# A two-layer decoder trunk: where the operands of its matmuls start in SBUF

## The chip, the cores and the metric

The kernel runs on one core of one Trainium2 chip. The metric is the time of one execution on the device, in microseconds (us). Before the change it took 2255.49 us, the median of three runs (2255.02 to 2256.84).

A core has five engines that work side by side and wait for each other by semaphores: TensorE (PE in the profile; its weight loads have a row of their own, PEld), VectorE (DVE), ScalarE (ACT), GpSimd (POOL) and SyncE (SP), which here only issues DMAs. Operands lie in SBUF, on-chip memory of 128 partitions; a tile occupies the same range of byte addresses in each partition. Matmul results go to PSUM.

## What is computed

Two layers, one sequence of 256 tokens, width 2048, everything in float32. Each layer is a token mixer (forgetting attention in layer 0, sliding-window attention in layer 1) and a gated ConvFFN, each with its input modulated by the conditioning vector and followed by a layer norm:

```python
for i in range(DEPTH):
    mod = c_act @ ada_w[i] + ada_b[i]
    sh1, sc1, g1, sh2, sc2, g2 = jnp.split(mod[:, None, :], 6, axis=-1)
    h = x * (1.0 + sc1) + sh1
    y = fox_attention(h, ...) if i % N_MIXERS == 0 else swa_attention(h, positions, ...)
    x = layer_norm(DEEPNORM_ALPHA * x + (1.0 + g1) * y, ln_mix_g[i], ln_mix_b[i])
    h = x * (1.0 + sc2) + sh2
    y = conv_ffn(h, ffn_w_up[i], ffn_conv_w[i], ffn_conv_b[i], ffn_w_down[i])
    x = layer_norm(DEEPNORM_ALPHA * x + (1.0 + g2) * y, ln_ffn_g[i], ln_ffn_b[i])
```

`conv_ffn` multiplies by `w_up` (2048 x 11264), convolves over three tokens, gates one half with the SiLU of the other, and multiplies by `w_down` (5632 x 2048). Nearly all of the work is in these products and in the projections into and out of the attentions.

## The kernel before

**Matmuls in three terms.** Each float32 operand is split into a rounded part (type float32r, which PE takes in one pass) and a residual: a = ah + al. A product is ah·bh + ah·bl + al·bh. For weights, ACT rounds a block `w` into `wh` (line 276) and DVE subtracts to get `wl` (line 287). The modulated input h lies transposed in one tile, `hHL`, 16 blocks of 128 rows, each with 256 columns of the rounded part and 256 of the residual (`hH`, `hL`). The gated values of the FFN lie in tiles `gT` of pool `gp`, and the attention's outputs in `oT`: blocks 0 to 11 in `gp`, blocks 12 to 15 in `hHL` itself, which is free by then (`o_tile`).

**A matmul has a stationary and a moving operand.** The stationary one (128 x 128, 512 bytes per partition) is loaded by a weight load, PEld; the moving one (256 or 512 columns, 1024 or 2048 bytes per partition) then streams past it. The load for the next matmul runs beside the present one. All go through `mm` (line 76). In a form like `wd<-hHL,wh` the name ahead of the arrow is the PSUM tile:

- `wd` (`w_stationary`, FFN up-projection): weights stationary, `hHL` moving. For each pair of 128-row blocks eight matmuls of 512 columns with `wh` (both halves of h at once) and then eight of 256 with `wl`. 22 column blocks of 512 and 8 pairs in each layer: 352 pairs.
- `ws` (`w_mm`, q and k of the first attention): weights stationary, `hHL` moving, 16 matmuls of 256 columns with `wh` and 8 with `wl` for each pair.
- `xs` (`x_mm`: v of the first attention, all of the second attention's input, the output projections, the FFN's down-projection): `hHL`, `oT` or `gT` stationary, weights moving; eight matmuls of 512 columns with `wh` and four with `wl` for each pair. The down-projection has 176 pairs, the two output projections 32 each, the second attention's input 40. The first attention's input has 96 pairs, two thirds of them `ws`; 45 of the 96 are in the opening.

Every pair streams 6144 columns.

**What sets the order.** The kernel's own planner issues a pair at a time: `stream` issues the load of `w` on SP's queue, the rounding on ACT and, up to two pairs ahead, the residual on DVE; after each pair `tick` lets background work take a step (the next layer's conditioning sums, attention heads, evacuations). The pools rotate: ten `w` tiles, four `wh`, four `wl`, 31 tiles in `gp`, four tiles of tag `t` (2 KB, for many short-lived things; `ttile`).

**Stages.** Opening (conditioning sums and the first attention's input, up to about 163 us), rest of the first attention (to 472), FFN of layer 0 (up, down, up, down: the FFN's columns go in two parts), second attention (1225 to 1505), FFN of layer 1, and the last layer norm.

**Addresses.** A pool is laid out in the order in which pools are opened, and within `cst` in the order in which its tiles are made. Before, this gave `hHL` a start 192 bytes past a multiple of 512 (a tile `gap` of 24 floats behind it holds the later pools in place), and `wh`, `wl`, `w` and everything in `gp` starts at multiples of 512. All slices that PE reads from these lie whole multiples of 512 bytes from the tile's start.

**Small loads on POOL.** `columns` loads the biases, the norms' parameters and the convolution's weights as rows into `t` tiles, PE transposes them, DVE copies them out. `rotary` loads the positions (`posr`), DVE casts them (`posf`), PE transposes them, and DVE and ACT make the sine tables for the second attention. `csil` is the SiLU of the conditioning vector, at the start.

Of the kernel before, what the change touches and what calls it, by code (L numbers as in the profile page):

```python
# [2 lines left out]

# [1 line left out]

# [5 lines left out]
F32 = mybir.dt.float32  # L11
# [30 lines left out]
def hybrid_trunk(ctx: ExitStack, tc: tile.TileContext, a: dict, out: bass.AP):  # L42
# [6 lines left out]
    cst = ctx.enter_context(tc.tile_pool(name="cst", bufs=1))  # L49
    wp = ctx.enter_context(tc.tile_pool(name="wp", bufs=10))  # L50
    hl = ctx.enter_context(tc.tile_pool(name="hl", bufs=4))
    gp = ctx.enter_context(tc.tile_pool(name="gp", bufs=31))
    tp = ctx.enter_context(tc.tile_pool(name="tp", bufs=4))
    sp = ctx.enter_context(tc.tile_pool(name="sp", bufs=4))
    psp = ctx.enter_context(tc.tile_pool(name="psp", bufs=8, space=bass.MemoryType.PSUM))

    def wtile(name="w"):
# [38 lines left out]
    adab = a["ada_b"].rearrange("l (r p) -> l r p", p=P)  # L96
    nc.sync.dma_start(rows0[:NADA, 1, :], adab[0])

    ident = cst.tile([P, P], F32, name="ident")
    nc.gpsimd.memset(ident, 0.0)  # L100
    nc.gpsimd.affine_select(out=ident, in_=ident, compare_op=ALU.not_equal, fill=1.0, base=0,
# [2 lines left out]
    nc.gpsimd.memset(ones, 1.0)  # L104

    mask = cst.tile([P, 3, P], F32, name="mask")
    nc.gpsimd.memset(mask, 0.0)
    nc.gpsimd.affine_select(out=mask[:, 1, :], in_=mask[:, 1, :], compare_op=ALU.is_gt, fill=NEG, base=0,
                            pattern=[[1, P]], channel_multiplier=-1)
    nc.gpsimd.affine_select(out=mask[:, 2, :], in_=mask[:, 2, :], compare_op=ALU.is_ge, fill=NEG, base=0,  # L110
                            pattern=[[-1, P]], channel_multiplier=1)

    sel = cst.tile([P, 2, FH], F32, name="sel")
# [6 lines left out]
    x = cst.tile([P, NT, D], F32, name="x")  # L120
    csil = cst.tile([KC, P], F32, name="csil")
    nc.scalar.activation(csil, rows0[:KC, 0, :], AF.Silu)
    cact = cst.tile([P, KC], F32, name="cact")
    pt = bank()
# [11 lines left out]
    sink = cst.tile([P, SQ], F32, name="sink")  # L136
    nsink = cst.tile([P, SQ], F32, name="nsink")
    sint = cst.tile([P, NT, HR], F32, name="sint")
    cost = cst.tile([P, NT, HR], F32, name="cost")

# [29 lines left out]
    def rotary():  # L170

        nc.gpsimd.dma_start(sink, a["swa_sinks"][0].partition_broadcast(P))
        posr = cst.tile([NT, P], I32, name="posr")
        nc.gpsimd.dma_start(posr, a["positions"].rearrange("b (t p) -> (b t) p", p=P))
        yield
        pin(nc.vector.tensor_scalar_mul(nsink, sink, -1.0))
        posf = cst.tile([NT, P], F32, name="posf")
        pin(nc.vector.tensor_copy(posf, posr))
# [24 lines left out]
        yield  # L203
        nc.scalar.activation(sint, ang, AF.Sin)
        nc.scalar.activation(cost, nturn, AF.Sin)
# [119 lines left out]
    def w_mm(ps, kc, h, l, last=KC - 1, first=0):  # L325

        cells = [(i, f, ps[f // 2][:, f % 2, :]) for i in range(2) for f in range(4)]
        for i, f, o in cells:
            wh = h[:, i, f * P:(f + 1) * P]
            mm(o, wh, hH[:, kc + i, :], start=kc + i == first and f % 2 == 0, skip_group_check=True)  # L330
            mm(o, wh, hL[:, kc + i, :], skip_group_check=True)
        for i, f, o in cells:
            mm(o, l[:, i, f * P:(f + 1) * P], hH[:, kc + i, :], stop=kc + i == last, skip_group_check=True)

    def x_stationary(wsrc, col, k0, nk, stat, end=0):

# [5 lines left out]
    def w_stationary(wsrc, col):  # L342

        ps = [bank("wd") for _ in range(4)]

        def use(kc, h, l):
            cells = [(i, f) for i in range(2) for f in range(4)]
            for i, f in cells:
                mm(ps[f], h[:, i, f * P:(f + 1) * P], hHL[:, kc + i].rearrange("p a s -> p (a s)"),
                   start=kc + i == 0)  # L350
            feed()
            for i, f in cells:
                mm(ps[f][:, :S], l[:, i, f * P:(f + 1) * P], hH[:, kc + i, :], stop=kc + i == KC - 1)

        stream(wsrc, 0, col, list(range(KC)), use)
        return ps
# [116 lines left out]
    def mod_pair(G, B, k, ps, fast=False):  # L473
        tmp = ttile()
        if fast:
            g, b = ([c[:, k + j:k + j + 1] for j in range(2)] for c in (G, B))
            o = [tmp[:, j * S:(j + 1) * S] for j in range(2)]
            high = lambda j: nc.scalar.activation(hH[:, k + j, :], ps[j], AF.Identity, bias=b[j], scale=g[j])
            whole = lambda j: pin(nc.vector.tensor_scalar(o[j], ps[j], g[j], b[j], op0=ALU.mult, op1=ALU.add))
            high(0), whole(1), high(1), whole(0)  # L480
            for j in range(2):
                pin(nc.vector.tensor_tensor(hL[:, k + j, :], o[j], f32(hH[:, k + j, :]), op=ALU.subtract))  # L482
# [4 lines left out]
        split(hH[:, k:k + 2, :], hL[:, k:k + 2, :], tmp.rearrange("p (j s) -> p j s", j=2))  # L487

    def hstat(kc, t):
        return hH[:, kc, t * P:(t + 1) * P], hL[:, kc, t * P:(t + 1) * P]  # L490

    onesr = ones.bitcast(F32R)

# [233 lines left out]
    def o_tile(kc):  # L727

        if kc >= KC - 4:
            return hH[:, kc, :], hL[:, kc, :]  # L730
        g = gtile("oT")
        return g[:, 0, :], g[:, 1, :]

# [28 lines left out]
    def fox(l, j):  # L762
# [16 lines left out]
        def forget_split():  # L779
            KH = KC // 2  # L780
            for q in range(2):
                src = wfs[0][:, q * KH:(q + 1) * KH, :].unsqueeze(2).broadcast_to([P, KH, P // FH, FH])
                h = hl.tile([P, 2, WB], F32R, tag="wh", name="fh")
                l = hl.tile([P, 2, WB], F32R, tag="wl", name="fl")
# [6 lines left out]
        def forget():  # L791
            lg = bank("lg")
            for kc in range(KC):
                wh, wl = fh[kc // 8][:, kc % 8, :], fl[kc // 8][:, kc % 8, :]
                mm(lg[:, :S], wh, hH[:, kc, :], start=kc == 0)
                mm(lg[:, :S], wh, hL[:, kc, :])
                mm(lg[:, :S], wl, hH[:, kc, :], stop=kc == KC - 1)
# [378 lines left out]
```

## Time and profile before

| | |
|---|---|
| median of three runs | 2255.49 us |
| the profiled execution's own time | 2256.26 us |
| its span, first to last instruction | 2254.5 us |
| mean granted TensorE clock | 0.996 |
| PE waiting for DVE or ACT, the longest totals by line | 4.7 us (`wh`), 4.3 us (`wl`) |
| PE waiting for DMA, total | 10.0 us, all in the opening |
| HBM read | 598.37 MB, 266 GB/s over the span |

"Busy" is the time from an instruction's start to its end. Matmuls overlap: one begins while the one before it is still draining, so the mean duration of a matmul is longer than what it costs in a row of them, and that cost is the spacing of their starts. The timeline merges equal neighbours into a row: its first number is the start of the first, the second the length of the whole row, and the count is at the end; the difference of two rows' starts is what the first row cost. It gives hundredths of a microsecond.

### The profile page before, as it was taken

To read this page: it belongs to the slowest core of one execution; us is meant where nothing else is said; L and a number is where in the kernel's file an instruction comes from. 1 tells how busy PE (TensorE), PEld (TensorE's weight loads), DVE (VectorE), ACT (ScalarE), POOL (GpSimd) and SP (SyncE) were. 2 spreads that over 40 slices of the span, in tenths; PEclk is the share of its full clock that TensorE was granted. 3 is DMA by queue.
4 is the path that set the end of the run, shared out by engine and by line. 5 is a ranking of instruction groups with operands and counts; after the bars stand their busy time and mean duration, and the time that the engine had idled before them with its cause. 6 is when DMAs were issued, how large, how long until landed. Compare 5 with 4: busy or idle time off the path is not lost. (4 is left out here: it accounts for less than half of the span.)

```text
span 2254.5 us, 33348 instructions
## 1 busy us (share of the span) xinstructions
PE 2203.2 (98%) x12196; PEld 1892.9 (84%) x12196; DVE 1852.2 (82%) x2685; ACT 1193.7 (53%) x1873; POOL 19.9 (1%) x51
## 2 busy tenths in 40 slices
PE   7999999999999999999999999999999999999997
PEld 6988898788888888888887788888888888888886
DVE  7989998889988968978978989889988655676766
ACT  4546544356555433555534578646655533555542
POOL 0000000000000000000000000000000000000000
PEclk9999999999999999999999999999999999999999
DMA  9999999869978889878887867678887556666553
GB/s 345 393 372 311 341 379 355 305 222 307 313 243 273 316 292 333 287 226 285 280 307 261 288 202 262 219 254 290 285 268 242 187 194 190 190 192 189 189 194 111
DMA packets 287285, 602.68 MB, mean 267 GB/s; under 512 B 21830, under 2 KB 55304, under 8 KB 286608
## 3 DMA queue, kind: packets, MB, share of 16 engines
q1 hardware_dynamic: 286064, 595.86, 77.8%
q0 software_dynamic: 1056, 4.69, 0.6%
q8 instruction: 95, 1.56, 0.3%
q14 instruction: 70, 0.57, 0.1%
HBM read 598.37 MB, written 2.10 MB: 266 GB/s over the span
## 5 line engine op out<-in xcount | busy, mean ns | idle before, releaser
L276 ACT CAST wh<-w 128x1024 fp32r<-128x1024 f32 x728 | 764.7, 1051 | 802.0 <-PE wd L76 267.5
L287 DVE TENSOR_TENSOR wl<-w,wh 128x1024 fp32r<-128x1024 f32 x728 | 887.0, 1221 | 297.0 <-ACT wh L276 283.7
L76 PE MATMUL wd<-hHL,wh 128*128 128x512 f32 x2816 | 717.9, 397 | 1.1 <-DVE hHL L482 1.1
L76 PEld LDWEIGHTS wd<-hHL,wh 128*128 128x128 f32 x2816 | 503.4, 188 | 100.1 <-issue 2.9
L76 PEld LDWEIGHTS wd<-hHL,wl 128*128 128x128 f32 x2816 | 373.3, 188 | 32.8 <-DVE wl L287 1.6
L76 PE MATMUL wd<-hHL,wl 128*128 128x256 f32 x2816 | 379.6, 277 | 1.1 <-DVE wl L287 1.1
L406 DVE SCALAR_TENSOR_TENSOR acc<-wa,cact,acc 128x1024 f32<-128x1024 f32 x300 | 380.2, 1277 | 0.0
L76 PE MATMUL xs<-wh,gT 128*128 128x512 f32 x1408 | 349.7, 390 | 0.0
L76 PEld LDWEIGHTS xs<-wh,gT 128*128 128x128 f32 x1408 | 263.4, 188 | 54.2
L76 PE MATMUL xs<-wl,gT 128*128 128x512 f32 x704 | 189.3, 389 | 0.0
L76 PE MATMUL xs<-wh,hHL 128*128 128x512 f32 x704 | 185.5, 400 | 2.9 <-DVE hHL L86 2.7
L76 PEld LDWEIGHTS xs<-wl,gT 128*128 128x128 f32 x704 | 132.1, 188 | 27.6
L76 PEld LDWEIGHTS xs<-wh,hHL 128*128 128x128 f32 x704 | 128.9, 190 | 29.1 <-DVE hHL L86 3.5
L76 PE MATMUL ws<-hHL,wh 128*128 128x256 f32 x1024 | 133.2, 282 | 7.1 <-ACT wh L276 4.7
L1066 ACT ACTIVATE u<-s,ccol 128x256 f32<-128x256 f32 x176 | 104.6, 599 | 66.5 <-DVE s L1061 48.8
L76 PEld LDWEIGHTS ws<-hHL,wh 128*128 128x128 f32 x1024 | 125.1, 190 | 11.0 <-ACT wh L276 6.2
L76 PE MATMUL xs<-wh,oT 128*128 128x512 f32 x384 | 99.8, 398 | 0.1
L76 PE MATMUL xs<-wl,hHL 128*128 128x512 f32 x352 | 97.0, 395 | 1.5 <-DVE wl L287 1.5
L551 DVE SCALAR_TENSOR_TENSOR oacc<-wo,cact,oacc 128x512 f32<-128x512 f32 x111 | 79.5, 746 | 15.1 <-DMA wo<-in_ada_w_dram 10.0
L1067 DVE SCALAR_TENSOR_TENSOR u<-s,ccol,u 128x255 f32<-128x255 f32 x176 | 84.0, 479 | 5.6 <-ACT u L1066 5.6
L1069 DVE SCALAR_TENSOR_TENSOR u<-s,ccol,u 128x254 f32<-128x254 f32 x176 | 83.8, 477 | 1.1
L76 PEld LDWEIGHTS xs<-wh,oT 128*128 128x128 f32 x384 | 70.7, 190 | 14.3 <-ACT pT L719 0.5
(223 smaller groups left out, 1643.1 us busy)
## 6 DMA issues: line engine op xcount, KB each, us to landing
w<-in_ffn_w_up_dram SPq DMA_DIRECT2D x352, 512.0 KB, 4.6
wa<-in_ada_w_dram SPq DMA_DIRECT2D x320, 512.0 KB, 5.1
w<-in_ffn_w_down_dram SPq DMA_DIRECT2D x176, 512.0 KB, 4.2
w<-in_fox_w_in_dram SPq DMA_DIRECT2D x96, 512.0 KB, 6.6
wo<-in_ada_w_dram SPq DMA_DIRECT2D x128, 256.0 KB, 6.7
w<-in_swa_w_in_dram SPq DMA_DIRECT2D x40, 512.0 KB, 5.4
w<-in_fox_w_o_dram SPq DMA_DIRECT2D x32, 512.0 KB, 5.8
w<-in_swa_w_o_dram SPq DMA_DIRECT2D x32, 512.0 KB, 5.4
```

The costliest lines, as they stand in the source:

```text
L76: return nc.tensor.matmul(o, lhsT, rhs, start=start, stop=stop, **kw)
L276: pin(nc.scalar.copy(h, w), False)
L287: pin(nc.vector.tensor_tensor(l, w, f32(h), op=ALU.subtract), go in behind)
L406: pin(nc.vector.scalar_tensor_tensor(ac, wo, cact[:, k:k + 1], ac, op0=ALU.mult, op1=ALU.add), True)
L551: nc.vector.scalar_tensor_tensor(ac, wk, cact[:, kc:kc + 1], ac, op0=ALU.mult, op1=ALU.add)
L1066: nc.scalar.activation(u, s, AF.Identity, bias=cw(CW, f), scale=cw(2, f))
L1067: nc.vector.scalar_tensor_tensor(u[:, 1:], s[:, :S - 1], cw(1, f), u[:, 1:], op0=ALU.mult, op1=ALU.add)
L1069: nc.vector.scalar_tensor_tensor(u[:, 2:], s[:, :S - 2], cw(0, f), u[:, 2:], op0=ALU.mult, op1=ALU.add)
```

## The change

The tiles that PE reads get other start addresses. Nothing else is computed, and no instruction is added or taken away. These are the starts as the two built programs have them, modulo 512 bytes:

| tile | before | after |
|---|---|---|
| `hHL` up to the end of the first attention | 192 | 192 |
| `hHL` from the first FFN on | 192 | 0 |
| `wh`, `fh` | 0 | 0 |
| `wl`, `fl` | 0 | 320 |
| `w`, `gT`, `oT` in `gp`, all of `gp` and tag `t` | 0 | 0 |
| `x` / `acc` / `gate` | 256 / 160 / 160 | 192 / 192 / 192 |
| `ident`, `ones`, `mask` | 128 | 0 |

`hHL` becomes a window on a tile `room` that is 48 floats (192 bytes) longer: `view(48)` at the start, `view(0)` ahead of each later modulation. The residual weights get a pool of their own, `hw`, between two paddings, and the small pool `sp` moves in front of it. To make room, `csil`, `posr` and `posf` no longer have tiles of their own in `cst`; they take turns in the four tiles of tag `t`.

```diff
+    sp = ctx.enter_context(tc.tile_pool(name="sp", bufs=4))
+    ctx.enter_context(tc.tile_pool(name="pad", bufs=1)).tile([P, 48], F32, name="pad")
+    hw = ctx.enter_context(tc.tile_pool(name="hw", bufs=4))
+    ctx.enter_context(tc.tile_pool(name="rest", bufs=1)).tile([P, 48], F32, name="rest")
     gp = ctx.enter_context(tc.tile_pool(name="gp", bufs=31))
...
+    room = cst.tile([P, KC * 2 * S + 48], F32R, name="hHL")
+    hv = SimpleNamespace()
+
+    def view(off):
+
+        hv.HL = room[:, off:off + KC * 2 * S].rearrange("p (k a s) -> p k a s", k=KC, a=2)
+        hv.H, hv.L = hv.HL[:, :, 0, :], hv.HL[:, :, 1, :]
+
+    view(48)
+    x = cst.tile([P, NT, D], F32, name="x")
+    for tag in ("acc", "gate"):
+        cst.tile([P, D], F32, tag=tag, name=tag)
...
-    csil = cst.tile([KC, P], F32, name="csil")
+    csil = ttile("csil")[:KC, :P]
...
-        posr = cst.tile([NT, P], I32, name="posr")
+        posr = ttile("posr")[:NT, :P].bitcast(I32)
...
-        posf = cst.tile([NT, P], F32, name="posf")
+        posf = ttile("posf")[:NT, :P]
...
+        cst.tile([P, 104], F32, name="gap")
...
-            l = hl.tile([P, 2, WB], F32R, tag="wl", name="wl")
+            l = hw.tile([P, 2, WB], F32R, tag="wl", name="wl")
...
-    hHL = cst.tile([P, KC, 2, S], F32R, name="hHL")
-    hH, hL = hHL[:, :, 0, :], hHL[:, :, 1, :]
-    cst.tile([P, 24], F32, name="gap")
...
     def between(l, v, g, b, name, ll):
...
         ada["held"] = False
+        view(0)
         modulate(*merged(l, v, g, b, ll), normalise)
```

Left out are the places where `hH`, `hL` and `hHL` become `hv.H`, `hv.L` and `hv.HL`, the pool of `fl`, which goes from `hl` to `hw` as that of `wl` does, and tiles of `cst` (`sel`, `sink`, `nsink`) that are made earlier.

On PE, DVE, ACT and SP every instruction stands where it stood. On POOL one row moves: the load of `posr`. Before, POOL's queue from the last constants of the opening to the convolution's rows reads:

```order
L117 AFFINE_SELECT sel<-sel 128x16 x2
L174 DMA posr<-in_positions_dram 2x128
L145 DMA rows<-in_ada_b_dram 96x128
L147 DMA rows<-in_ln_mix_g_dram 32x128
L147 DMA rows<-in_ln_mix_b_dram 32x128
L147 DMA rows<-in_ln_ffn_g_dram 32x128
L147 DMA rows<-in_ln_ffn_b_dram 32x128
L807 MEMSET ze 128x256
L161 DMA rows<-in_ffn_conv_w_dram 88x128 x3
L162 DMA rows<-in_ffn_conv_b_dram 88x128
L813 MEMSET Bm 128x256
```

With the change the same stretch of POOL's queue reads as follows (the line numbers are those of the changed file):

```order
L135 AFFINE_SELECT sel<-sel 128x16 x2
L160 DMA rows<-in_ada_b_dram 96x128
L162 DMA rows<-in_ln_mix_g_dram 32x128
L162 DMA rows<-in_ln_mix_b_dram 32x128
L162 DMA rows<-in_ln_ffn_g_dram 32x128
L162 DMA rows<-in_ln_ffn_b_dram 32x128
L820 MEMSET ze 128x256
L189 DMA posr<-in_positions_dram 2x128
L826 MEMSET Bm 128x256
L176 DMA rows<-in_ffn_conv_w_dram 88x128 x3
L177 DMA rows<-in_ffn_conv_b_dram 88x128
```

The load of `posr` has gone from behind the constants to behind the memset of `ze`, and the memset of `Bm` now stands ahead of the first convolution rows. Two waits change with it. DVE's cast of `posr` (line 178 before), in an unchanged place in DVE's queue, waits for a load that is issued later. And the first four convolution rows now go into the `t` tile that the biases and norm parameters were in, so their loads wait until PE has transposed those (lines 151 and 155 before); before, they had a `t` tile that was free.

More of the change, by code (lines that the diff above doesn't have):

```diff
@@ L2 @@
 from contextlib import ExitStack
+from types import SimpleNamespace
 import numpy as np
@@ L97, in hybrid_trunk @@
     nc.sync.dma_start(rows0[:NADA, 1, :], adab[0])
+    sel = cst.tile([P, 2, FH], F32, name="sel")
+    sink = cst.tile([P, SQ], F32, name="sink")
+    nsink = cst.tile([P, SQ], F32, name="nsink")
     ident = cst.tile([P, P], F32, name="ident")
@@ L111, in hybrid_trunk @@
                             pattern=[[-1, P]], channel_multiplier=1)
-    sel = cst.tile([P, 2, FH], F32, name="sel")
     nc.gpsimd.memset(sel, 0.0)
@@ L135, in hybrid_trunk @@
     ccol = cst.tile([P, DEPTH, CW + 1, NF], F32, name="ccol")
-    sink = cst.tile([P, SQ], F32, name="sink")
-    nsink = cst.tile([P, SQ], F32, name="nsink")
     sint = cst.tile([P, NT, HR], F32, name="sint")
@@ L329, in w_mm @@
             wh = h[:, i, f * P:(f + 1) * P]
-            mm(o, wh, hH[:, kc + i, :], start=kc + i == first and f % 2 == 0, skip_group_check=True)
-            mm(o, wh, hL[:, kc + i, :], skip_group_check=True)
+            mm(o, wh, hv.H[:, kc + i, :], start=kc + i == first and f % 2 == 0, skip_group_check=True)
+            mm(o, wh, hv.L[:, kc + i, :], skip_group_check=True)
         for i, f, o in cells:
-            mm(o, l[:, i, f * P:(f + 1) * P], hH[:, kc + i, :], stop=kc + i == last, skip_group_check=True)
+            mm(o, l[:, i, f * P:(f + 1) * P], hv.H[:, kc + i, :], stop=kc + i == last, skip_group_check=True)
     def x_stationary(wsrc, col, k0, nk, stat, end=0):
@@ L348, in use @@
             for i, f in cells:
-                mm(ps[f], h[:, i, f * P:(f + 1) * P], hHL[:, kc + i].rearrange("p a s -> p (a s)"),
+                mm(ps[f], h[:, i, f * P:(f + 1) * P], hv.HL[:, kc + i].rearrange("p a s -> p (a s)"),
                    start=kc + i == 0)
@@ L481, in mod_pair @@
             for j in range(2):
-                pin(nc.vector.tensor_tensor(hL[:, k + j, :], o[j], f32(hH[:, k + j, :]), op=ALU.subtract))
+                pin(nc.vector.tensor_tensor(hv.L[:, k + j, :], o[j], f32(hv.H[:, k + j, :]), op=ALU.subtract))
             return
@@ L486, in mod_pair @@
                                 op0=ALU.mult, op1=ALU.add)
-        split(hH[:, k:k + 2, :], hL[:, k:k + 2, :], tmp.rearrange("p (j s) -> p j s", j=2))
+        split(hv.H[:, k:k + 2, :], hv.L[:, k:k + 2, :], tmp.rearrange("p (j s) -> p j s", j=2))
     def hstat(kc, t):
-        return hH[:, kc, t * P:(t + 1) * P], hL[:, kc, t * P:(t + 1) * P]
+        return hv.H[:, kc, t * P:(t + 1) * P], hv.L[:, kc, t * P:(t + 1) * P]
     onesr = ones.bitcast(F32R)
@@ L729, in o_tile @@
         if kc >= KC - 4:
-            return hH[:, kc, :], hL[:, kc, :]
+            return hv.H[:, kc, :], hv.L[:, kc, :]
         g = gtile("oT")
@@ L783, in forget_split @@
                 h = hl.tile([P, 2, WB], F32R, tag="wh", name="fh")
-                l = hl.tile([P, 2, WB], F32R, tag="wl", name="fl")
+                l = hw.tile([P, 2, WB], F32R, tag="wl", name="fl")
                 ho, lo = (i.rearrange("p a (k r f) -> p (a k) r f", r=P // FH, f=FH) for i in (h, l))
@@ L794, in forget @@
                 wh, wl = fh[kc // 8][:, kc % 8, :], fl[kc // 8][:, kc % 8, :]
-                mm(lg[:, :S], wh, hH[:, kc, :], start=kc == 0)
-                mm(lg[:, :S], wh, hL[:, kc, :])
-                mm(lg[:, :S], wl, hH[:, kc, :], stop=kc == KC - 1)
+                mm(lg[:, :S], wh, hv.H[:, kc, :], start=kc == 0)
+                mm(lg[:, :S], wh, hv.L[:, kc, :])
+                mm(lg[:, :S], wl, hv.H[:, kc, :], stop=kc == KC - 1)
             yield
```

6 lines of the change are left out of this document (2 added, 4 removed).

## Prediction

> **What bounds the kernel now.** I read the page's busy shares first, then the stages (busy time in windows), then the tensor engine's groups of instructions, and last its timeline at the places where matmuls of different operands follow each other.
>
> ```profile
> PE 2203.2 (98%) x12196; PEld 1892.9 (84%) x12196; DVE 1852.2 (82%) x2685; ACT 1193.7 (53%) x1873; POOL 19.9 (1%) x51
> ```
>
> PE is busy for 98% of a span of 2254.5 us, so the span is the sum of what the matmuls take, wherever they follow each other without a hole. The windows say where that is (PE, PEld, DVE, ACT, POOL busy; granted clock; DMA share and GB/s):
>
> ```profile
> 20.00:163.00 143.00, 135.88 (x979) 126.19 (x978) 123.54 (x171) 73.87 (x93) 2.52 (x5) 0.99 1.06 383
> 163.00:420.00 257.00, 250.23 (x1665) 226.42 (x1665) 240.38 (x346) 140.07 (x248) 5.29 (x11) 1.00 0.95 345
> 475.00:747.00 272.00, 271.04 (x1558) 234.32 (x1558) 248.45 (x351) 158.21 (x241) 0.00 (x0) 1.00 0.84 283
> 747.00:881.00 134.00, 134.00 (x608) 111.40 (x608) 110.17 (x114) 54.89 (x61) 0.00 (x0) 1.00 0.88 317
> ```
>
> The opening (20 to 163 us) moves data without pause (share 1.06). The two FFN stages shown (up-projection, then down-projection) are PE without a hole, at full clock, with DVE at 91% and 82%. The idle column of the next rows says the same of all four up and four down stages (1.1 and 0.0 us over all their wh matmuls), so a nanosecond per matmul there is a nanosecond of the span. Now the matmuls themselves:
>
> ```profile
> L76 PE MATMUL wd<-hHL,wh 128*128 128x512 f32 x2816 | 717.9, 397 | 1.1 <-DVE hHL L482 1.1
> L76 PE MATMUL xs<-wh,gT 128*128 128x512 f32 x1408 | 349.7, 390 | 0.0
> L76 PE MATMUL xs<-wh,hHL 128*128 128x512 f32 x704 | 185.5, 400 | 2.9 <-DVE hHL L86 2.7 <-ACT hHL L85 0.2
> ```
>
> Three groups do the same work, 128x512 against 128x128 weights, and one takes 390 ns and the others 397 and 400. Durations overlap, so I take the spacing of starts, from the timeline in the second up stage (a "pair" is two 128-row blocks: eight matmuls with wh, eight with wl):
>
> ```profile
> 1001.71 2.02 PE L76 MATMUL wd<-hHL,wh 128*128 128x512 f32 x8
> 1003.57 1.07 PE L76 MATMUL wd<-hHL,wl 128*128 128x256 f32 x8
> 1004.48 2.02 PE L76 MATMUL wd<-hHL,wh 128*128 128x512 f32 x8
> ...
> 1010.03 1.32 PE L76 MATMUL wd<-hHL,wh 128*128 128x512 f32 x5
> ```
>
> 1001.71 to 1010.03 is three pairs, 2.773 us each: 1.86 for the wh group, 0.91 for the wl group. A down pair streams the same 6144 columns (8+4 matmuls of 512):
>
> ```profile
> 746.03 1.07 PE L76 MATMUL wd<-hHL,wl 128*128 128x256 f32 x8
> 746.94 1.99 PE L76 MATMUL xs<-wh,gT 128*128 128x512 f32 x8
> 748.77 1.07 PE L76 MATMUL xs<-wl,gT 128*128 128x512 f32 x4
> 749.68 1.98 PE L76 MATMUL xs<-wh,gT 128*128 128x512 f32 x8
> 751.49 1.07 PE L76 MATMUL xs<-wl,gT 128*128 128x512 f32 x4
> ...
> 755.12 1.07 PE L76 MATMUL xs<-wh,gT 128*128 128x512 f32 x4
> ```
>
> 749.68 to 755.12 is two pairs, 2.72 us each. So an up pair carries 0.053 us that a down pair doesn't, all of it in the wh group (1.86 against 1.81). What differs is where the operands start: I call **distance** the start of the stationary slice less that of the moving one, modulo 512 bytes. It is 320 in the up stages (0 less 192), 0 in the down stages, 192 in the attention's xs matmuls. The reading I go by is that a weight load, which runs beside the matmul before it, meets that matmul's reads at some distances.
>
> **The change part by part.**
>
> *Up stages.* wh goes from distance 320 to 0; wl keeps 320 (320 less 0). At distance 0 the wh group has two prices in the trace: 1.81 in a run of its own kind, and 1.83 when it follows a wl group of the up stage (746.94 to 748.77 above: exactly the neighbour that it will have in every pair). I take 1.83, and 0.91 for wl, whose distance doesn't change: a pair is 2.74, and 352 pairs (2816 matmuls by eight) save 352 x 0.033 = **11.7 us**. The best is 2.72 (18.7 us). The worst is a wl group that doesn't settle, as the same form does in the first attention:
>
> ```profile
> 240.56 2.05 PE L76 MATMUL ws<-hHL,wh 128*128 128x256 f32 x16
> 242.44 1.10 PE L76 MATMUL ws<-hHL,wl 128*128 128x256 f32 x8
> 243.39 0.22 PE L76 MATMUL S<-Bm,A 128*128 128x128 f32 x1
> ...
> 290.96 1.98 PE L76 MATMUL ws<-hHL,wh 128*128 128x256 f32 x16
> ...
> 293.68 1.98 PE L76 MATMUL ws<-hHL,wh 128*128 128x256 f32 x16
> ```
>
> 242.44 to 243.39 is 0.95 for eight: a pair of 1.83 + 0.95 = 2.78, 352 x 0.007 = 2.5 us lost. (The whole ws pair took 2.83 there, and 2.72 from 290.96 to 293.68: the same matmuls at the same distance, unsettled and settled.)
>
> *Down stages.* wh stays at 0; wl, now the moving operand at 320 with gT at 0, goes from 0 to 192. The trace has matmuls of 512 columns at 192, and the way into and out of it:
>
> ```profile
> 1247.48 1.99 PE L76 MATMUL xs<-wh,hHL 128*128 128x512 f32 x8
> ...
> 1252.98 1.99 PE L76 MATMUL xs<-wh,hHL 128*128 128x512 f32 x8
> ...
> 1450.54 1.08 PE L76 MATMUL xs<-wl,hHL 128*128 128x512 f32 x4
> 1451.45 2.00 PE L76 MATMUL xs<-wh,oT 128*128 128x512 f32 x8
> 1453.29 1.07 PE L76 MATMUL xs<-wl,oT 128*128 128x512 f32 x4
> ...
> 1472.38 1.08 PE L76 MATMUL xs<-wl,hHL 128*128 128x512 f32 x4
> 1473.29 1.98 PE L76 MATMUL xs<-wh,oT 128*128 128x512 f32 x8
> 1475.10 1.07 PE L76 MATMUL xs<-wl,oT 128*128 128x512 f32 x4
> ```
>
> 1247.48 to 1252.98 is two pairs at 192 throughout, 2.75 each, so a third of the 0.03 falls to four matmuls: 0.01. The first wh group after leaving 192 took 1.84 once and 1.81 once. So a down pair becomes 2.72 at best and 2.76 at worst; I take 2.735, the middle, since the two exits are equally good rows: 176 pairs (1408 by eight) x 0.015 = **2.6 us lost** (0 to 7.0).
>
> *Output projections.* Their 64 pairs mix oT in gp (distance 0 before) with the last four blocks in hHL. 48 pairs read gp and lose as a down pair does: 48 x 0.015 = **0.7 us** (0 to 1.9).
>
> *Second attention.* 40 input pairs go from 192 throughout (2.75) to wh at 0 and wl at 192 (2.735): **0.6 us saved** (0.4 lost to 1.2 saved).
>
> *First attention.* hHL stays at 192, so wh keeps its distances; wl goes to 128 (ws) and 384 (xs), which no row shows. The opening's 45 pairs lie under its DMAs. The other 51 are bounded by the settled and unsettled ws pairs, 2.72 and 2.83; their mix now lies between, so I take 0.02 each, 51 x 0.02 = **1.0 us lost**, between 51 x -0.02 and 51 x 0.05 (1.0 saved, 2.6 lost).
>
> *Buffers of tag t.* csil, posr and posf now take turns in the four t buffers. On POOL the load of posr moves from 3.9 us to behind the memset of ze, and the convolution rows wait until the transposes of the earlier rows leave their buffer.
>
> ```profile
> 188.81 0.32 POOL L807 MEMSET ze<- 128x256 f32 x1 [32.11 <-DVE ze L806]
> 189.06 1.56 POOL L161 DMA_DIRECT2D rows<-in_ffn_conv_w_dram  x3
> ...
> 191.13 0.27 PE L155 MATMUL sm<-ident,rows 128*128 128x128 f32 x1
> ...
> 193.76 0.27 DVE L178 CAST posf<-posr 2x128 f32<-2x128 int32 x1
> ...
> 197.16 0.47 PE L166 MATMUL sm<-ident,rows 88*128 88x88 f32 x4
> ...
> DMA to landing us min/median/max: 4.4/5.2/6.3
> ...
> L951 DVE TENSOR_TENSOR r<-kv,sint x2: 191/222/252, 1254.3 to 1257.5; 128x32 f32<-128x32 f32 x2
> ```
>
> posr will be issued at about 189.1 and land 4.4 to 6.3 us later (the line before last: the loads of rows between 185 and 200 us), 193.5 to 195.4, where DVE wants it at 193.76: DVE stands 0 to 1.6 us, with two residuals (wl) queued behind it. The four convolution rows are issued from 191.4 on, 0.52 apart, the last at 193.0, and land by 197.4 to 199.3; PE's transposes want them at 197.16, and every matmul queues behind those: **1.1 us lost** at the median (0.2 to 2.2), the DVE stand lying inside it. The sine tables that posr leads to are first read at 1254.3 (last line), and the second set of rows is asked for later than the first.
>
> *At nothing:* DVE and ACT on moved tiles. DVE took 687 ns for t<-xs,gate and 686 for x<-x,t at quite different offsets:
>
> ```profile
> L621 DVE TENSOR_TENSOR t<-xs,gate 128x512 f32<-128x512 f32 x48 | 32.8, 687 | 33.0 <-PE xs L76 32.8
> L622 DVE TENSOR_TENSOR x<-x,t 128x512 f32<-128x512 f32 x48 | 32.7, 686 | 0.4
> ```
>
> They lie beside PE; the first up stage leaves DVE 9% of slack, and a saving of 1.2% on PE uses an eighth of that. If that cover were gone, the first up stages (176 pairs) would save nothing, 5.8 us. The order of PE, DVE, ACT and SP is unchanged.
>
> **Sum:** -11.7 + 2.6 + 0.7 - 0.6 + 1.0 + 1.1 = -6.9 us. The profiled execution took 2256.3 (span 2254.5 and 1.8 around it), which gives 2249.4; the median of the runs shown, 2255.5, lies 0.8 below it, and I state the forecast against it: **2248.6 us**, 0.3% faster.
>
> **Rivals.**
>
> *The layout isn't the cause.* The 0.05 us could belong to the alternation of 512 and 256 columns in the up stages, not to addresses. For it: up and down pairs differ in that too. Against it: xs<-wh,hHL and xs<-wh,gT differ in nothing but the tile, and take 2.75 and 2.72. The time would be 2255.5 + 1.1 = 2256.6. The Trainium skill speaks for this rival: "SBUF — State Buffer", section "Who interferes with whom", gives PE two independent read ports and says that PE never waits on anyone. By that rule no address could matter and the sum would be the 1.1 us alone; the trace's 2.75 against 2.72 disagrees.
>
> *Every group settles at once.* Up pairs at 2.72, no loss elsewhere: -18.7 - 1.2 + 1.1, 2236.7. For it: 1473.29, where a group left 192 at no cost. Against it: 746.94 and 1451.45.
>
> *Slower: the mixed distances never settle.* One mechanism, at the seam between wh and wl of each pair: every change of distance unsettles the groups behind it. Up pairs 2.78 (+2.5), down pairs 2.76 (+7.0), output projections +1.9, first attention +2.6, second attention +0.4, rows +1.1: 2271.0. It decides against the change once an up pair saves less than half of what a down pair loses, since there are 352 against 176. For it: 242.44, and 1451.45. Against it: wl of the up stages settles today behind wh groups that meet it.
>
> *The floor falls too.* "TensorE: Matmul & The Clock Gate", section "Back-to-back issue gap", of the Trainium skill has N/2.4 + 2.5 ns, 215.8 for 512 columns and 109.2 for 256. That would make an up pair 2.60 us; the fastest pair of this trace, with everything at distance 0, takes 2.72. From rows: if the pair that is now freed fell below 2.72 by as much again as it stands above it (0.053), 352 pairs would give 37 us in all and 2218.
>
> **How the numbers follow.** Forecast and its neighbourhood (3 to 11 us faster) 0.45; layout not the cause 0.20; all settled 0.16; never settled 0.16; floor 0.03. The likeliest case's own range is 2244 to 2253. Eight in ten: I leave out the floor and the outer halves of the two settled cases, 2239 to 2263. A measurement of this kernel tells about 0.2% (4.5 us) from no change: faster is most of the forecast's share (0.37), with all settled and the floor, 0.56; same is layout-not-the-cause and the forecast's near edge, 0.28; slower 0.16.
>
> **What would show it.** Right: wh groups of the up stages spaced 1.83, not 1.86, their mean duration near 390; wl groups at 0.91; down pairs at 2.72 to 2.76 with the excess in wl and the wh matmuls just behind; a hole on PE at the transposes of the convolution rows near 197 us. Wrong: wh groups still at 1.86 (rival one), wl groups at 0.95 (rival three), or DVE's residuals releasing PE in the first up stage.

## The result, and the profile after

The changed kernel takes 2269.37 us (median of four runs, 2269.12 to 2269.82); the kernel before, run beside it, 2255.85. The ratio is 1.0059, with a 95% interval from 1.0047 to 1.0071. It is 0.6% slower, where 0.3% faster was forecast, and it lies above the range of 2239 to 2263.

The page of the changed kernel has PE as busy as before, 98%, in a span of 2267.6 us that is 13.1 longer:

```profile
PE 2218.1 (98%) x12196; PEld 1904.6 (84%) x12196; DVE 1852.6 (82%) x2685; ACT 1193.3 (53%) x1873; POOL 20.0 (1%) x51
```

So the added time lies in the matmuls, not in holes between them. PE's largest groups (busy time, mean ns of one, and idle time before them with its releaser):

```profile
L80 PE MATMUL wd<-hHL,wh 128*128 128x512 f32 x2816 | 709.6, 393 | 1.1 <-DVE hHL L495 1.1
L80 PE MATMUL wd<-hHL,wl 128*128 128x256 f32 x2816 | 390.1, 281 | 1.1 <-DVE wl L303 1.1
L80 PE MATMUL xs<-wh,gT 128*128 128x512 f32 x1408 | 353.6, 392 | 0.0
```

The group that was meant to be freed, `wd<-hHL,wh`, did get shorter, 393 ns where it had 397. The `wh` group of the down stages got longer, 392 for 390, though its operands lie exactly as they lay. Groups that share a pair have become dearer with no wait added: the idle time, the last column, was 1.1, 1.1 and 0.0 before too. The timeline of an up stage (start, duration, engine, group and count) gives the spacing:

```profile
1020.35 2.00 PE L80 MATMUL wd<-hHL,wh 128*128 128x512 f32 x8
1022.19 1.11 PE L80 MATMUL wd<-hHL,wl 128*128 128x256 f32 x8
1023.13 2.00 PE L80 MATMUL wd<-hHL,wh 128*128 128x512 f32 x8
```

The `wh` group is spaced 1.84 (1.86 before), the `wl` group 0.94 (0.91 before): a pair of **2.78**, against 2.773 before and 2.74 in the forecast. And a down stage:

```profile
799.12 2.00 PE L80 MATMUL xs<-wh,gT 128*128 128x512 f32 x8
800.96 1.10 PE L80 MATMUL xs<-wl,gT 128*128 128x512 f32 x4
801.90 2.00 PE L80 MATMUL xs<-wh,gT 128*128 128x512 f32 x8
...
804.67 2.00 PE L80 MATMUL xs<-wh,gT 128*128 128x512 f32 x8
```

799.12 to 804.67 is two pairs of **2.775** (2.72 before, 2.735 in the forecast). Of the 0.055, 0.03 falls to the `wl` group, which left distance 0, and the rest to the `wh` group, which stayed there.

From the starts of each stage's first matmul in the two traces, the 13.1 us come from these places:

| | before | after | difference | forecast |
|---|---|---|---|---|
| all ahead of the first up stage | 472.5 | 474.3 | +1.8 | +2.1, and part of the projections' 0.7 |
| four up stages | 996.7 | 998.7 | +2.0 | -11.7 |
| four down stages, to the end | 505.4 | 514.0 | +8.6 | +2.6 |
| second attention and its output projection | 279.9 | 280.6 | +0.7 | -0.6, and the rest of the 0.7 |

The forecast is 20 us off: 13.7 of them in the up stages, 6.0 in the down stages.

### The profile page after: what moved, and what is told of

The parts are those of the page before. It is cut to its first block, busy times and chain, and to the rows that moved or that the text cites. A ratio compares the mean times of both kernels' runs of the same rounds, so it can differ in the third digit from the quotient of the medians.

```text
span 2267.6 us, 33351 instructions
## 1 busy us (share of the span) xinstructions
PE 2218.1 (98%) x12196; PEld 1904.6 (84%) x12196; DVE 1852.6 (82%) x2685; ACT 1193.3 (53%) x1873; POOL 20.0 (1%) x51
## 5 line engine op out<-in xcount | busy, mean ns | idle before, releaser
L80 PE MATMUL wd<-hHL,wh 128*128 128x512 f32 x2816 | 709.6, 393 | 1.1 <-DVE hHL L495 1.1
L80 PEld LDWEIGHTS wd<-hHL,wl 128*128 128x128 f32 x2816 | 381.5, 189 | 27.9 <-DVE wl L303 1.6
L80 PE MATMUL wd<-hHL,wl 128*128 128x256 f32 x2816 | 390.1, 281 | 1.1 <-DVE wl L303 1.1
L80 PE MATMUL xs<-wl,gT 128*128 128x512 f32 x704 | 194.2, 396 | 0.0
```

Of the source, the lines that this page charges most:

```text
L80: return nc.tensor.matmul(o, lhsT, rhs, start=start, stop=stop, **kw)
```

## Experiments

The theory after the result: what a pair costs depends on its two distances together, that of the `wh` group and that of the `wl` group, written (d1, d2) from here on, and on nothing else in the kernel. The rivals: tiles that DVE, ACT or the DMAs touch at new places slow PE's reads; or it is the buffers of tag t and the loads on POOL.

### Matmuls alone (m1_map)

The trunk's computation is left out. After one load, PE runs matmuls of the trunk's shapes on one tile, with nothing beside them: first at a single distance (`p?` of 512 columns, 24 at each step of 32 bytes), then up pairs (`u??`) and down pairs (`d??`), each four times, with d1 and d2 on a grid of 64 bytes from 0 (`a`) to 448 (`h`). In the down pairs the moving operand moves and the stationary one stays, as in the trunk.

```python
for k in range(8): mm(ps, sta(k, 64 * a), mov(k // 4, 512), 512, ...)
for k in range(8): mm(ps, sta(8 + k, 64 * b), mov(k // 4, 256), 256, ...)
```

> A kernel of matmuls alone, no weights streaming in and no other engine at work: runs of 24 matmuls of 512 and of 256 columns at 16 distances (start of the stationary slice less that of the moving one, modulo 512, in steps of 32 bytes), then groups as in an up pair (8 of 512 columns at one distance, 8 of 256 at another, four times over) and as in a down pair (8 of 512 at one, 4 of 512 at another), for all 8 x 8 distances in steps of 64 bytes. It leaves out the trunk's computation. Theory (the two reads of PE meet, by distance, with a memory from group to group): spacing depends on the distance alone; 512 columns at 0 0.227 us each, at 192 0.229, at 320 0.233; up pair (320, 320) 2.773, (0, 320) 2.780; down pair (0, 0) 2.72, (0, 192) 2.773. Rival (PE's reads meet those of DVE, ACT or the DMAs): no dependence on the distance here, 2.72 for every pair. Rival (it is the absolute address, not the distance): the down pairs, where the moving operand starts elsewhere, and the up pairs, where the stationary one does, give different maps.

The timeline of this kernel at single distances (0, 32, 64, then 256, 288):

```profile
18.31 5.61 PE L44 MATMUL pa<-room 128*128 128x512 f32 x24
23.76 5.75 PE L44 MATMUL pb<-room 128*128 128x512 f32 x24
29.35 5.76 PE L44 MATMUL pc<-room 128*128 128x512 f32 x24
...
62.86 5.61 PE L44 MATMUL pi<-room 128*128 128x512 f32 x24
68.31 5.75 PE L44 MATMUL pj<-room 128*128 128x512 f32 x24
```

From start to start, 24 matmuls take 5.45 us at distance 0, 5.59 at 32, and 5.45 again at 256. **The period is 256 bytes, not 512.** Over the last twelve matmuls of each run that is 226.7 ns at 0, 229 at 192 and 233 at most others. The pairs (four from one row's start to the next; `uaf` is (0, 320), `ufc` is (320, 128)):

```profile
156.51 11.34 PE L44 MATMUL uaa<-room 128*128 128x512 f32 x64
167.69 11.29 PE L44 MATMUL uab<-room 128*128 128x512 f32 x64
...
212.34 11.29 PE L44 MATMUL uaf<-room 128*128 128x512 f32 x64
223.46 11.39 PE L44 MATMUL uag<-room 128*128 128x512 f32 x64
...
436.10 11.16 PE L44 MATMUL udb<-room 128*128 128x512 f32 x64
447.10 11.36 PE L44 MATMUL udc<-room 128*128 128x512 f32 x64
...
625.47 11.41 PE L44 MATMUL ufc<-room 128*128 128x512 f32 x64
636.72 11.37 PE L44 MATMUL ufd<-room 128*128 128x512 f32 x64
...
659.17 11.27 PE L44 MATMUL uff<-room 128*128 128x512 f32 x64
670.27 11.41 PE L44 MATMUL ufg<-room 128*128 128x512 f32 x64
...
871.06 11.05 PE L44 MATMUL daa<-room 128*128 128x512 f32 x48
881.95 11.21 PE L44 MATMUL dab<-room 128*128 128x512 f32 x48
...
904.02 11.25 PE L44 MATMUL dad<-room 128*128 128x512 f32 x48
915.10 11.07 PE L44 MATMUL dae<-room 128*128 128x512 f32 x48
```

`uff` takes 11.10 for four, 2.775 each: the up stage before. `uaf` takes 2.78: the up stage after. `daa` takes 2.72 and `dad` 2.77: the down stage before and after. With no other engine at work, the pairs cost what they cost in the trunk, so the first rival falls. The rival of the absolute address falls too: a down pair at (64, 64) or (192, 192), where the moving operand was moved, comes to 233.3 and 228.8 ns a matmul (a twelfth of the pair below), as the runs do in which the stationary one was moved. The whole map, ns a pair, as the mean of the second and third of the four repeats (rows d1, columns d2, up to 192; the cells that are equal to these modulo 256 differ from them by 6 ns at most, and by up to 14 in the two at (192, 0)):

```text
up    0    64   128   192      down   0    64   128   192
  0  2792  2780 2806  2784        0  2720  2766 2754  2772
 64  2810  2779 2813  2803       64  2794  2800 2794  2787
128  2804  2780 2806  2789      128  2784  2787 2788  2786
192  2780  2746 2806  2762      192  2758  2760 2759  2746
```

Two entries settle it. In the column d2 = 64, where `wl` stood before and after, freeing `wh` from 64 to 0 gives 2780 for 2779, and 2780 for 2774 in the fourth repeat, when (64, 64) has settled: no gain, and some 6 ns lost. And an up pair with **everything at distance 0 costs 2792**, more than the one that was to be freed; only a down pair is cheapest there.

### The change with one part undone (e1, e2, e3)

e1_wl_at_0 puts `wl` back at 0 and leaves the rest of the change:

```diff
-    ctx.enter_context(tc.tile_pool(name="pad", bufs=1)).tile([P, 48], F32, name="pad")
+    ctx.enter_context(tc.tile_pool(name="pad", bufs=1)).tile([P, 96], F32, name="pad")
-    ctx.enter_context(tc.tile_pool(name="rest", bufs=1)).tile([P, 48], F32, name="rest")
```

> The changed kernel with the residual weights back at multiples of 512; all else as changed (the input at 0 from the first FFN on, at 192 in the first attention). Distances: up pairs (0, 0), down pairs (0, 0). Theory (distance with a memory): down pairs go back from 2.773 to 2.72, 176 x 0.053 = 9.3 us less than the changed kernel; up pairs are 2.72 if 256 columns settle at distance 0 (352 x 0.060 = 21 us less, 2238 in all, faster than before by 0.8%), and 0.95 for the wl group, 2.76 or more, if they don't (about 2254). Rival (the loss comes from the input at 0, not from the residual weights at 320): down pairs stay at 2.773 and the time near 2269.

It took 2262.03 us, 1.0027 of the kernel before (1.0017 to 1.0037). Its timeline in the second up and the first down stage:

```profile
1021.92 2.00 PE L79 MATMUL wd<-hHL,wh 128*128 128x512 f32 x8
1023.76 1.11 PE L79 MATMUL wd<-hHL,wl 128*128 128x256 f32 x8
1024.71 2.00 PE L79 MATMUL wd<-hHL,wh 128*128 128x512 f32 x8
...
798.88 1.98 PE L79 MATMUL xs<-wh,gT 128*128 128x512 f32 x8
...
801.60 1.98 PE L79 MATMUL xs<-wh,gT 128*128 128x512 f32 x8
```

The down pair is 2.72 again. So moving `wl` is what cost the down stages their 0.055, the `wh` group's share of it included. The up pair is (0, 0) now and takes 2.79, as the map has it. The expectation missed here: its second case had the `wl` group at 0.95, as it came, but a pair of 2.76 or more and about 2254 us, which is 0.95 and a `wh` group at 1.81; behind this `wl` group the `wh` group costs 1.84. Aligning all operands of the FFNs loses as well.

e2_input_at_192 undoes the other half: the modulated input stays at 192 throughout, and `wl` stays moved, so up pairs are (64, 128).

```diff
-        view(0)
```

> The changed kernel without the step of the input to 0 (it stays at 192 throughout); the residual weights at 320. Distances: up pairs (320, 128), down pairs (0, 192) as in the changed kernel. Theory (distance with a memory): down pairs stay at 2.773; the wh groups of the up pairs go back to 1.86, and wl at distance 128 takes 0.91 to 0.95, so up pairs 2.77 to 2.81 and the time 2266 to 2280. Rival (the loss comes from the input at 0): down pairs at 2.72, time back near 2256.

2279.32 us, 1.0107 (1.0092 to 1.0122), the slowest of all:

```profile
1021.45 2.02 PE L80 MATMUL wd<-hHL,wh 128*128 128x512 f32 x8
...
1024.27 2.02 PE L80 MATMUL wd<-hHL,wh 128*128 128x512 f32 x8
```

2.82 a pair; the map has 2.813. By the stages' starts, the four down stages take 505.1 us in e1 and 514.1 in e2, for 505.4 before and 514.0 after: in these kernels they follow `wl` alone. For the whole kernel, the move of `wl` by itself costs 23 us, and that of the input on top of it gains 10; but the input's move by itself is e1, and it costs 6 (each with the buffers of tag t). The parts don't add, since the price belongs to the pair.

e3_own_posr gives `posr` its own tile, so that it is loaded at the start again:

```diff
-        posr = ttile("posr")[:NT, :P].bitcast(I32)
+        posr = cst.tile([NT, P], I32, name="posr")
```

> The changed kernel with the positions back in a tile of their own, so that their load stands early on POOL again; no start address changes modulo 512. Theory (the buffers of tag t cost 1.1 us, by the wait for the convolution rows and the positions near 197 us): the start of the first up stage 0.5 to 2 us earlier than the 474.3 of the changed kernel, everything behind it unchanged. Rival (the 1.8 us that the first attention lost are matmul spacing too): the start stays within 0.5 us of 474.3.

2268.81 us in the one run, 0.6 under the median of the changed kernel and 0.3 under its lowest run: not told apart from it. The first up stage starts at 473.89, 0.4 us earlier, which is within what the rival allows. PE still waits for the convolution's rows, 0.43 us:

```profile
200.22 0.89 PE L181 MATMUL sm<-ident,rows 88*128 88x88 f32 x4 [0.43 <-DMA rows<-in_ffn_conv_w_dram]
```

So the late `posr` isn't where the time went: DVE's cast of it stands at 196.12 us here, with the early load, and at 196.13 in the changed kernel, with the late one. The wait for the convolution's rows isn't undone by this run. One tile fewer takes its turn in the buffers, so the first of these rows now wait for DVE's work on `ze`, and their load is issued at 195.08 (194.18 in the changed kernel).

### The period in the trunk (e4), and a finer map (m2)

If 256 is the period, `wl` at 64 modulo 512 is `wl` at 320 under another name:

```diff
-    ctx.enter_context(tc.tile_pool(name="pad", bufs=1)).tile([P, 48], F32, name="pad")
+    ctx.enter_context(tc.tile_pool(name="pad", bufs=1)).tile([P, 112], F32, name="pad")
-    ctx.enter_context(tc.tile_pool(name="rest", bufs=1)).tile([P, 48], F32, name="rest")
+    ctx.enter_context(tc.tile_pool(name="rest", bufs=1)).tile([P, 112], F32, name="rest")
```

> The changed kernel with wl at 64 instead of 320 modulo 512; nothing else moves. Period 256 (the map of matmuls alone): nothing changes, up pairs 2.780, down pairs 2.773, 2269 us within 2. Period 512, on which the prediction was built: wl's distances become new ones in the up stages (64 for 320), the down stages (448 for 192) and the first attention, so pairs change by some 10 ns or more and the time by over 4 us in one direction or the other.

2268.34 us, 1.0056 (1.0041 to 1.0071): the same time, with pairs of 2.78 and 2.77. The period holds in the trunk.

m2_map leaves out the trunk's computation too, and asks what the price belongs to: runs in steps of 16 bytes, stationary slices of 32, 64 and 96 columns (`x?`, `y?`, `z?`, at 0, 64, 128, 192), and the pairs, three of each, on a grid of 32 bytes (64 for the ws pairs `w??`).

> Matmuls alone again, the trunk's computation left out: pure runs in steps of 16 bytes (512 and 256 columns), runs of 512 columns with stationary slices of 32, 64 and 96 columns, and pairs of wh and wl groups on a finer grid of distances. If the price belongs to the weight load (128 columns read in a burst beside the matmul before), a narrower load meets the same matmul for less time: at 32 columns the excess over the price at distance 0 falls from about 6.5 ns to a quarter, 1.6 ns or less. If it belongs to the starts alone (first words of both reads in one bank), it stays near 6.5 ns at every width. The seam theory expects that no pair of unequal distances (d1 for wh, d2 for wl, not equal modulo 256) reaches 2720, and that the best pair off the (0,0) of the down stages stays at 2740 to 2750. Steps of 16 bytes: if the rule is about whole 32-byte steps, 16 bytes cost what 0 or 32 do, 226.7 or 233 ns; if every offset but 0 costs, all lie at 229 to 234.

```profile
155.87 5.72 PE L62 MATMUL xa<-room 128*32 128x512 f32 x24
161.43 5.72 PE L62 MATMUL xb<-room 128*32 128x512 f32 x24
166.99 5.71 PE L62 MATMUL xc<-room 128*32 128x512 f32 x24
...
1338.43 8.64 PE L44 MATMUL wbb<-room 128*128 128x256 f32 x72
1346.91 8.61 PE L44 MATMUL wbc<-room 128*128 128x256 f32 x72
1355.35 8.34 PE L44 MATMUL wbd<-room 128*128 128x256 f32 x72
1363.53 8.73 PE L44 MATMUL wca<-room 128*128 128x256 f32 x72
```

Both answers were wrong. With 32 columns to load, 24 matmuls take 5.56 at distance 0 and 5.56 at 64: the price is there at every distance, 228 to 233 ns for each narrow width, and the free case at 0 is gone. The price isn't in proportion to what a load reads, and it isn't decided by the starts alone. What the reads do to each other remains **open**. The other answers: 16 bytes off costs 226.7 as 0 does, and so does 240; from 32 to 224 a run costs 229 to 234. No up or down pair but the down pair (0, 0) reached 2720, and the best up pair was (192, 64) with 2747. Of the ws pairs two did, against what was expected of unequal distances: (64, 192) takes 8.18 us for three above, 2.720 once it repeats, and (192, 64) 2.720 from the start (from 1405.96 to 1414.12 for three).

The ws pair that the kernel before runs, (64, 64), is where map and trunk part: three take 8.48 above, 2.827 each, and in the trunk one takes 2.72 where it follows its own kind (290.96 to 293.68 in the prediction). For these pairs the map of matmuls alone doesn't hold, and no run here shows why. One difference left untested is where the results go: the map's pair writes one range of PSUM, the trunk's writes several.

### Choosing by the map (f1, f2)

If the map is right, it must find a better layout. f1_views starts from the kernel before, with all weights and `gT` at 0, and moves the modulated input alone between stages: 192 in the first attention, 320 for the FFNs (up pairs (192, 192)), 256 in the second attention (xs pairs at 0).

```diff
-    hHL = cst.tile([P, KC, 2, S], F32R, name="hHL")
-    cst.tile([P, 24], F32, name="gap")
+    room = cst.tile([P, KC * 2 * S + 32], F32R, name="hHL")
+    cst.tile([P, 120], F32, name="gap")
...
         ada["held"] = False
+        view(32 if v else 16)
         modulate(*merged(l, v, g, b, ll), normalise)
```

> The kernel before with all weights and gated values at 0 and the modulated input alone moved between stages, at 192 in the first attention (as before), at 320 for the FFNs and at 256 in the second attention. The map of matmuls alone gives an up pair at distance 192 2762 ns instead of 2773, a down pair unchanged at 2720, and an xs pair of the second attention at distance 0 2720 instead of 2747: 352 x 0.011 + 40 x 0.027 = 3.9 + 1.1 = 5.0 us less, about 2250.8, faster than both kernels. Rival one, that the loss of the change came from elsewhere (tiles that other engines read and write at new places): 2255.9, no change. Rival two, that only an equal distance in all of PE's stages settles: up pairs stay at 2773, 2254.8.

2251.01 us (2249.27 to 2253.11, 11 runs), 0.9978 (0.9970 to 0.9987): faster than both kernels, and 0.2 from the time expected, in part by luck (see below). Its up stage:

```profile
1019.77 1.99 PE L77 MATMUL wd<-hHL,wh 128*128 128x512 f32 x8
...
1022.55 2.00 PE L77 MATMUL wd<-hHL,wh 128*128 128x512 f32 x8
...
1025.29 1.99 PE L77 MATMUL wd<-hHL,wh 128*128 128x512 f32 x8
...
1028.06 2.00 PE L77 MATMUL wd<-hHL,wh 128*128 128x512 f32 x8
```

Pairs of 2.78 and 2.74 alternate. The same instructions on the same distances cost one or the other, and the map's (192, 192) does so too, with the same addresses in each repeat (2784, 2741, 2772 ns): so it is what ran ahead that decides. The four up stages take 991.3 us by their starts, 5.4 under before where 3.9 was expected; the second attention with its output projection saves 0.3 where 1.1 was expected. The two misses nearly cancel.

f2_both_views moves `wl` too: at 128 modulo 256 in the up stages, which makes their pairs (192, 64), and in the ws matmuls, (64, 192); at 0 elsewhere.

```diff
+    def wltile(name, at):
+        t = hl.tile([P, 2 * WB + 32], F32R, tag="wl", name=name)
+        o = (at - 32 * int(("0110" if turn[0] < 49 else "0011")[turn[0] % 4])) % 64
+        turn[0] += 1
+        return t[:, o:o + 2 * WB].rearrange("p (k f) -> p k f", k=2)
...
-            l = hl.tile([P, 2, WB], F32R, tag="wl", name="wl")
+            l = wltile("wl", at)
```

(The four buffers stand 128 bytes apart modulo 512; the digits are the buffers' turns. `posf` moves into the tile of `csil` to make room.)

> As f1_views, and wl a view that moves too: at distance 64 modulo 256 in the up stages, where wh stays at 192, at 192 in the first attention's ws matmuls, where wh stays at 64, and as in f1_views elsewhere. The maps of matmuls alone give 2746 to 2747 ns for the up pair (192, 64), against 2760 on average in f1_views and 2773 before, and a settled 2720 for the ws pair (64, 192), which costs 2720 to 2912 in the trace of before by what ran ahead of it. Second attention and down stages as in f1_views. Up: 352 x 0.0265 = 9.3 us under before, second attention 1.1, ws pairs 0 to 2.5: about 2244, some 7 us under f1_views. Rival: what settles in a long run of one pair doesn't in the trunk (other stages and feeds between), up pairs stay at 2760: 2250 to 2251, the time of f1_views.

2246.7 us (2246.03 to 2248.55, five runs), 0.9963 (0.9949 to 0.9977), the fastest here, and 2.7 over the time expected:

```profile
1022.34 2.00 PE L77 MATMUL wd<-hHL,wh 128*128 128x512 f32 x8
...
1025.08 2.00 PE L77 MATMUL wd<-hHL,wh 128*128 128x512 f32 x8
...
1027.83 2.00 PE L77 MATMUL wd<-hHL,wh 128*128 128x512 f32 x8
```

2.745 a pair without alternation, as the map says. The up stages take 988.5, 8.2 under before, where 9.3 was expected. The ws pairs gave nothing: four in a row take 2.72 at (64, 64) in f1 and at (64, 192) in f2, and those among other matmuls up to 2.92 in both, once 3.00 in f1. The map had 2.827 and 2.720 for the two: for these pairs it is no guide to the trunk. The first up stage starts at 471.2 in f2 and 473.2 in f1, though, with no difference in those pairs to explain it. Some 1.1 us of this is there from PE's first wait for a load, which ends at 11.64 in f2 and at 12.77 in f1; for the rest, single profiles scatter there by 1.2 us (472.5 to 473.7 among the three kernels with the distances of before, e1 and f1 among them).

## Why the prediction was wrong

**What bounds the kernel: right.** PE without a hole, and a nanosecond per pair is a nanosecond of the span. The address as the cause was right too. The rival that layout isn't the cause had the same pairs cost the same anywhere; the map shows 2720 to 2800 for one down pair by its distances alone. The Trainium skill, "SBUF — State Buffer", "Who interferes with whom", by which PE's two read ports are independent, spoke for that rival. The 226.7 against 233 ns of the map, with no other engine at work, disagrees.

**Up stages: the step that failed.** "I take 1.83, and 0.91 for wl, whose distance doesn't change." The first half held (1.84). The second took the price of a group for a property of its own distance. It belongs to the sequence: `wl` at 64 (320 is 64 modulo 256) costs 0.91 behind `wh` at 64 and 0.94 behind `wh` at 0; the map's pairs, 2774 once settled and 2780, agree. What `wh` gained, `wl` gave back: 352 x 0.007 = 2.5 us lost where 11.7 were to be gained (352 x 0.033 is 11.6), and 2.0 lost by the stages' starts. The row that showed it stood in the prediction: 242.44, `wl` at 0.95. It was priced as the worst case, and set aside because `wl` of the up stages "settles today behind wh groups that meet it". Why it settles there the map doesn't tell: one distance for both isn't enough, since (0, 0) costs 2792.

**Down stages: the same error, and a size.** 2.735 came from rows at 192 throughout, with a third of their excess for the `wl` group, and one of two exits at a cost. Measured is 2.775, above the worst case of 2.76. Neither row held a pair that goes from 0 to 192 and back each time; that seam costs 0.055, most of it new, and 176 pairs lose 9.7 by that, 8.6 by the stages' starts.

**Rival three came nearest,** "the mixed distances never settle", 2271.0 for a measured 2269.4, and at its place, the seam between `wh` and `wl`. Up pairs came at its 2.78; down pairs were worse than its 2.76 and the first attention milder than its 2.6. The two rows that it had for itself, 242.44 and 1451.45, were the ones that held. Its reason, that a change of distance unsettles the groups behind it, fits the down pairs, but not the up pairs: (0, 0), with no change, costs 2792 and more than (0, 64), and (192, 64), with one, costs least. That the time came so near is partly luck, since some of its terms were too low and others too high. The condition on which it decides, an up pair saving less than half of what a down pair loses, was met by an up pair that saved nothing.

**First attention, second attention, projections.** In the second attention, pairs that follow their own kind take 2.77 for 2.75 (its input, (0, 192) after) and 2.77 for 2.72 (the output projection): the same seam as in the down stages, and 0.7 lost in all where the input was to save 0.6. "The opening's 45 pairs lie under its DMAs" doesn't hold between waits, where these pairs are spaced by their distances as any others are. Two stretches of the opening, before and after:

```profile
147.71 1.99 PE L76 MATMUL ws<-hHL,wh 128*128 128x256 f32 x16
...
150.45 1.98 PE L76 MATMUL ws<-hHL,wh 128*128 128x256 f32 x16
...
153.17 1.99 PE L76 MATMUL xs<-wh,hHL 128*128 128x512 f32 x8
```

```profile
149.27 2.05 PE L80 MATMUL ws<-hHL,wh 128*128 128x256 f32 x16
...
152.11 1.99 PE L80 MATMUL ws<-hHL,wh 128*128 128x256 f32 x16
...
154.88 2.03 PE L80 MATMUL xs<-wh,hHL 128*128 128x512 f32 x8
```

Two ws pairs take 5.46 before and 5.61 after. What of this reaches the span is within the scatter of single profiles. PE's wait for `wh` near 128 us alone lasts from 1.6 to 4.2 us in the eight traces of the trunk; e2, with the distances of the change in the first attention, comes to its first up stage at 473.55, and e1, with those of before, at 473.69. The 1.8 us in the table can't be told apart by its parts.

**Buffers of tag t: over-sized.** 1.1 us forecast; the transposes at 199.63 start without a wait and take 0.83 us for 0.47 before, 0.36 more, because the load of the third one's operand waits for its rows.

```profile
199.63 0.83 PE L181 MATMUL sm<-ident,rows 88*128 88x88 f32 x4
200.00 0.32 PEld L181 LDWEIGHTS sm<-ident,rows 88*128 88x128 f32 x2 [0.21 <-DMA rows<-in_ffn_conv_w_dram]
```

PE came there 2.5 us later than before (197.16), so the rows had more time to land. PE's next long wait, for ACT's `pr` near 220 us, is 2.41 us before and 1.84 after, so the 0.36 is taken up there: PE stands 2.4 us later than before behind that wait (220.99 for 218.63), as it did ahead of the transposes.

**The floor** stayed where the trace had it: no pair below 2720 in either map, 226.7 ns a matmul.

## What to carry to other kernels

Price a layout by the whole repeating sequence of matmuls, measured in one small kernel of that sequence: the cost of a group at its own distance, read from a run of its own kind, doesn't carry over to a mix. Here a map of matmuls alone gave the trunk's up and down pairs to within some nanoseconds and found a layout 0.4% faster than the kernel before, where the rule "same distance, no conflict" lost in both forms tried, for the `wh` groups of the up stages alone (the change) and for all operands of the FFNs (e1). Check the map against the trunk's own rows before going by it: for the ws pairs of the first attention it was off by 0.1 us a pair.

## What the runs showed of the hardware

- In a run of their own kind, matmuls of 512 float32r columns against 128 are spaced 226.7 ns when the starts of stationary and moving operand are equal modulo **256** bytes (within 16), and 229 to 234 otherwise; no other engine is needed for it, and it makes no difference which of the two operands is moved.
- For 256 columns distance 0 is no better than others: 120 ns there in a run of their own, 116.7 to 120 at most others. 113.3, half of 226.7, comes only in some states: at 64 a run took 113.3 in one map (m2) and 117.8 in the other, behind different runs.
- The spacing remembers. Pairs of one kind alternate between 2.74 and 2.77 in f1, and in down pairs the `wh` group at distance 0 costs 1.81 behind a `wl` group at 0 and 1.84 behind one at 192.
- With 32, 64 or 96 stationary columns, 512 moving ones are spaced 228 to 233 ns at every distance, 0 included.
